# Shifting priorities by a table in a list-scheduled decoder layer, and a matmul price fitted to the measured rate

## The chip, the cores and the metric

The kernel runs on one core of one Trainium2 chip. The metric is device microseconds (us) of that core. The time before is the median of three timed runs; the profile comes from one further execution, whose own time is named beside its span below.

## The reference, cut to what matters

One decoder layer works on 1024 tokens of width 1024, with 16 learned tokens in front of them. Everything is float32. Four parallel branches (causal pooling, latent attention, a Conformer convolution, a short gated convolution) are merged by sigmoid gates.

```python
h = rms_norm(h_res, pre_norm_g[i])
z = h @ w_in[i]                         # 1024 -> 7328 columns, split among the branches
...
y_b = (mla_attention(...) * silu(mg)) @ w_out_mla[i]     # 8 heads, causal softmax
m = gts[0]*y_a + gts[1]*y_b + gts[2]*y_c + gts[3]*y_d
h_res = h_res + rms_norm(m @ w_o[i], post_norm_g[i])
return h_res[:, N_META:]
```

## The kernel before, in words

**Precision.** Each float32 operand is split into a high part, which TensorE can take, and a low rest (`split`: ScalarE copies, GpSimd or VectorE subtracts). A product is three matmuls: high by high, high by low, low by high. The two large products (`w_in` and `w_o`) are done by seven block products in place of eight.

**Three stages.** Stage one computes `z` and runs the convolution, pooling and the attention's inputs beside it. Stage two is attention (`maxima`, `attend`, `head_out`) in 16 units: 8 heads by 2 halves of the tokens. Between its matmuls stand 48 fills (`fills`, L1679): each is six matmuls of another branch's output product into a bank `y` of PSUM, followed on VectorE by a gating step that writes `th` and an addition to the running sum `m`. Stage three is the output: the attention branch's own output product (bank `u`, operand `boM`), then the product with `w_o`, whose results get a square on ScalarE, a gain multiply, a mean and a power on VectorE and GpSimd, and two closing VectorE operations per block of 128 tokens (`final`, L1899) before they are stored.

**In a unit of attention** (`attend`, L1583), each of 5 or 9 blocks of keys takes three matmuls into one of five banks `s`, a mask addition on VectorE on the diagonal, an exponential into `p32` and a copy into `pt` on ScalarE, a subtraction into `pt` on GpSimd (the low part), and three matmuls into the one bank `o`. At the end ScalarE copies bank `o` to `ol`. The row maxima of a later unit (`row_maxima`) also use the banks `s`; VectorE reduces them into `mxs`. `head_out` (L1660) scales `ol`, gates it and splits it into `boM`.

**What sets the order.** Nothing is issued while the program is written down. `record` (L324) stores each operation with its inputs' writers, a price from `cost` (L300) and a priority: its position in the record, less whatever `ahead` has lifted. The fills have their position plus 400. At the end of each stage `flush` (L363) plays the stage through: five engines, each of which, when free, starts the ready operation of the lowest priority number for which buffers are free; a price after that its results are due. In this order the instructions are then issued, and the chip's engines run them strictly in that order, each waiting for what it needs. So neither price nor priority changes what is computed; they change the order in which each engine, and each DMA queue, gets its instructions. In stage one, where the play finds TensorE idle, it also puts in small transposes that nobody reads (`keep_busy`).

The price of a matmul before is (L311):

```python
max(108, n / 2.25 + 3)        # n columns, in ns; also for a transpose
```

Of the kernel before, what the change touches and what calls it, by code (L numbers as in the profile page):

```python
# [21 lines left out]
F32 = mybir.dt.float32  # L22
# [191 lines left out]
class Plan:  # L214
# [6 lines left out]
    WAKE = {"PE": 350, "ACT": 150, "DVE": 150, "POOL": 150, "SP": 0}  # L221

    def __init__(self, nc):
        self.nc, self.ops, self.todo, self.lift, self.pipe = nc, [], [], 0, None
        self.after = 0
# [73 lines left out]
    @staticmethod  # L299
    def cost(eng, op, outs, ins, pow_):  # L300
        def size(v):
            return math.prod(v.shape[1:])
        if op == "dma_start":
            v, w = outs[0], ins[0]
            n = math.prod(v.shape) * 4
            run = 4 * min(v.shape[-1], w.shape[-1])
            return {"SP": 450, "ACT": 350, "POOL": 1000}[eng], n * (0.0235 + 35 / run) / 16
        n = max(size(v) for v in outs + [v for v in ins if isinstance(v, View)])
        if eng == "PE":
            n = size(outs[0])  # L310
            return (max(108, n / 2.25 + 3) if op == "transpose" or ins[0].dtype != F32 else max(430, 1.7 * n)), 0  # L311
        psum = any(isinstance(v, View) and v.buf.psum for v in outs + ins)
        if eng == "ACT":
            return (160 + 0.857 * n if psum else 200 + 0.83 * n), 0
        if op in ("memset", "affine_select"):
            return (60 if op == "memset" else 180) + 0.85 * n, 0
        if eng == "POOL":
            return (500 + 140 * n if pow_ else 180 + 2.2 * n), 0
        if op == "reciprocal":
            return 150 + 8.5 * n, 0  # L320
        both = psum and outs[0].buf.psum
        return 142 + (1.2 if op == "scalar_tensor_tensor" and (both or not psum) else 1.07) * n, 0
# [37 lines left out]
            return v.real() if isinstance(v, View) else v  # L360
        getattr(self.handle[o["eng"]], o["op"])(*map(real, o["args"]), **{k: real(v) for k, v in o["kw"].items()})  # L361

    def flush(self):  # L363

        self.lay_out()
        self.pipe = None
        ready = {e: [] for e in self.free}
        events, order = [], []
        for o in self.todo:
            o["need"] = 0  # L370
            o["at"] = 0
            for j in o["deps"]:
                d = self.ops[j]
                if d["end"] is None:
                    d["users"].append(o)
                    o["need"] += 1
                else:
                    o["at"] = max(o["at"], d["end"])
        for o in self.todo:
            if not o["need"]:  # L380
                heapq.heappush(events, (o["at"], 0, o["i"]))
        for e, t in self.free.items():
            heapq.heappush(events, (t, 1, 0))
        groups = {id(b.group): b.group for o in self.todo for b in o["bufs"] if b.group}
        for g in groups.values():
            for sl in g["slots"]:
                if sl["after"]:
                    heapq.heappush(events, (sl["after"], 1, 0))

        def slot(b, t):  # L390

            free = [sl for sl in b.group["slots"] if not sl["live"] and sl["after"] <= t]
            if free and (b.group["any"] or b.group["order"][b.group["next"]] is b):
                return min(free, key=lambda sl: (sl["after"], sl["i"]))

        def fits(o, t):

            if o["op"] == "dma_start" and o["eng"] != "POOL" and len(self.landed) >= 8 and self.landed[-8] > t:
                return False
            return all(slot(b, t) for b in o["bufs"] if not b.live and b.group)  # L400

        while events:
            t = events[0][0]
            while events and events[0][0] <= t:
                _, kind, i = heapq.heappop(events)
                if kind == 0:
                    o = self.ops[i]
                    bisect.insort(ready[o["eng"]], (o["prio"], o["i"]))
                elif kind == 2:
                    for b in self.ops[i]["bufs"]:  # L410
                        b.left -= 1
                        if b.left == 0 and b.group:
                            b.slot["live"], b.slot["after"] = None, t
            for e in self.free:
                if self.free[e] > t:
                    continue
                o = next((self.ops[i] for _, i in ready[e] if fits(self.ops[i], t)), None)
                if o is None:
                    if e == "PE" and self.idle and self.ops[self.idle[1]]["end"] is None:
                        self.row += 1  # L420
                        if self.row <= 8:
                            order.append(self.idle[0])
                        self.free[e] = t + 160
                        heapq.heappush(events, (self.free[e], 1, 0))
                    continue
                ready[e].remove((o["prio"], o["i"]))
                for b in o["bufs"]:
                    if not b.live:
                        b.live = True
                        if b.group:  # L430
                            b.slot = slot(b, t)
                            b.slot["live"] = b
                            b.group["next"] += 1
                o["start"] = t
                if e == "PE":
                    self.row = 0
                if o["turns"]:
                    o["cost"] += max(0, self.port[{"DVE": "POOL", "POOL": "DVE"}[e]] - t) * 0.7
                    self.port[e] = t + o["cost"]
                self.free[e] = t + o["cost"]  # L440
                o["end"] = t + o["cost"] + self.WAKE[e] + o["late"]
                if o["op"] == "dma_start":
                    if self.pipe is None:
                        self.pipe = max((x["done"] for x in self.ops if x["op"] == "dma_start"
                                         and "done" in x and x["start"] <= t), default=0)
                    o["done"] = self.pipe = max(self.pipe, t) + o["bytes"]
                    land = self.pipe + o["bytes"] + 4500 + min(0, o["extra"])
                    o["end"] = land + max(0, o["extra"])
                    if o["eng"] != "POOL":
                        self.landed.append(land)  # L450
                    heapq.heappush(events, (land, 1, 0))
                for b in o["bufs"]:
                    b.last = max(b.last, o["end"])
                order.append(o)
                heapq.heappush(events, (self.free[e], 1, 0))
                heapq.heappush(events, (o["end"], 2, o["i"]))
                for u in o["users"]:
                    u["need"] -= 1
                    same = u["eng"] == e and o["op"] != "dma_start"
                    u["at"] = max(u["at"], self.free[e] if same else o["end"])  # L460
                    if not u["need"]:
                        heapq.heappush(events, (u["at"], 0, u["i"]))
        if len(order) < len(self.todo):
            raise RuntimeError("no order: " + str([(o["eng"], o["op"], o["i"]) for o in self.todo if "start" not in o][:5]))
        for o in order:
            self.issue(o)
        self.todo = []


@with_exitstack  # L470
def trunk_kernel(ctx, tc, a):
# [10 lines left out]
    def ld(out, in_):  # L482
        SP.dma_start(f(out) if out.dtype == F32R else out, f(in_) if in_.dtype == F32R else in_)
# [13 lines left out]
    def split(hi, lo, src, eng=None):  # L497
        copy(hi, src)
        sub(eng or POOL, lo, src, f(hi))
# [1520 lines left out]
```

## Time and profile before

| | us |
|---|---|
| median of the three timed runs (965.73 to 969.6) | 968.28 |
| the profiled execution, its own time | 959.63 |
| its span | 957.9 |

TensorE works at a mean granted clock of 0.997. The stages, as the instructions show them: products with `w_in` and what runs beside them to about 629.5 us, attention to about 829.5 us, the output to the end. How to read the profile: PE is TensorE's matmuls and PEld its weight loads, which run ahead of the matmuls; DVE is VectorE, ACT ScalarE, POOL GpSimd, and SPq the queue that issues most DMAs. Matmuls are pipelined, so each record is longer than the distance from one start to the next. Nearly all operations carry line L361, the line in `issue` that hands them over, so groups are told apart by the tiles they write and read (`ps_s` is a bank `s`).

### The profile page before, as it was taken

To read this page: it belongs to the slowest core of one execution; us is meant where nothing else is said; L and a number is where in the kernel's file an instruction comes from. 1 tells how busy PE (TensorE), PEld (TensorE's weight loads), DVE (VectorE), ACT (ScalarE), POOL (GpSimd) and SP (SyncE) were. 2 spreads that over 40 slices of the span, in tenths; PEclk is the share of its full clock that TensorE was granted. 3 is DMA by queue.
4 is the path that set the end of the run, shared out by engine and by line. 5 is a ranking of instruction groups with operands and counts; after the bars stand their busy time and mean duration, and the time that the engine had idled before them with its cause. 6 is when DMAs were issued, how large, how long until landed. Compare 5 with 4: busy or idle time off the path is not lost.

```text
span 957.9 us, 15219 instructions
## 1 busy us (share of the span) xinstructions
PE 943.9 (99%) x4945; PEld 804.2 (84%) x4945; DVE 720.2 (75%) x1124; ACT 453.5 (47%) x925; POOL 677.7 (71%) x627
## 2 busy tenths in 40 slices
PE   8999999999999999999999999999999999999996
PEld 8998999988888888888888888888878878788885
DVE  6856979996999799547583657337778888799857
ACT  7752343434444445544454543266556565225632
POOL 5957669668787768669775977466467686738955
PEclk9999999999999999999999999999999999999998
DMA  8146566676779886788686678798978663783543
GB/s 262 46 126 198 151 202 196 211 224 204 249 229 280 281 283 209 244 224 245 221 255 187 191 243 279 220 300 259 294 207 275 199 184 111 264 266 107 189 141 144
DMA packets 143876, 205.96 MB, mean 215 GB/s; under 512 B 21169, under 2 KB 88752, under 8 KB 143028
## 3 DMA queue, kind: packets, MB, share of 16 engines
q1 hardware_dynamic: 134820, 188.20, 63.9%
q10 hardware_dynamic: 8656, 15.74, 4.5%
q8 instruction: 39, 0.64, 0.3%
q0 software_dynamic: 320, 1.05, 0.3%
q14 instruction: 41, 0.34, 0.1%
HBM read 132.01 MB, written 72.89 MB: 214 GB/s over the span
## 4 chain that ended last, share of the span: by engine, by line
PE 92%; DVE 3%; POOL 2%; issue 1%; ACT 1%; DMA 1%; SPq 0%; DVEq 0%; POOLq 0%; ACTq 0%
PE ps_pa L361 17%; PE ps_pb L361 17%; PE ps_pc L361 16%; PE ps_o L361 9%; PE ps_pd L361 8%; PE ps_u L361 7%; PE ps_s L361 7%; PE ps_y L361 6%; PE ps_x L361 4%; DMA x<-in_x_dram 1%; DVE th L361 1%; POOL pt L361 0%; ACT junk L361 0%; DVE op L361 0%; DVE c L361 0%
## 5 line engine op out<-in xcount | busy, mean ns | idle before, releaser
L361 PE MATMUL ps_pa<-B,A 128*128 128x512 f32 (+2 forms) x792 | 171.9, 359 | 0.0
L361 PE MATMUL ps_pb<-T,S 128*128 128x512 f32 (+2 forms) x792 | 170.7, 358 | 0.2 <-DVE u L361 0.2
L361 PEld LDWEIGHTS ps_pb<-T,S 128*128 128x128 f32 x792 | 134.4, 189 | 22.4 <-DVE u L361 0.4
L361 PEld LDWEIGHTS ps_pa<-B,A 128*128 128x128 f32 x792 | 134.2, 188 | 21.2 <-issue 0.2
L361 POOL TENSOR_TENSOR S<-ss,S 128x512 fp32r<-128x512 f32 x84 | 116.4, 1398 | 50.1 <-ACT S L361 43.3
L361 POOL TENSOR_TENSOR pt<-p,pt 128x512 fp32r<-128x512 f32 (+1 forms) x96 | 102.2, 1089 | 53.3 <-PE ps_s L361 27.4
L361 POOL TENSOR_TENSOR A<-raw,A 128x512 fp32r<-128x512 f32 x84 | 114.3, 1370 | 36.0 <-ACT A L361 35.7
L361 DVE TENSOR_TENSOR u<-ps_pb,u 128x512 f32<-128x512 f32 (+2 forms) x66 | 40.2, 610 | 67.3 <-PE ps_pb L361 62.2
L361 DVE SCALAR_TENSOR_TENSOR ps_w<-conv,par,ps_w 128x512 f32<-128x512 f32 x116 | 87.2, 752 | 2.5
L361 PE MATMUL ps_y<-bo,whl 128*128 128x512 f32 x288 | 84.6, 404 | 0.2 <-DVE th L361 0.2
L361 PE MATMUL ps_pd<-T,A 128*128 128x512 f32 (+2 forms) x396 | 84.5, 358 | 0.0
L361 PE MATMUL ps_pc<-T,S 128*128 128x512 f32 (+1 forms) x396 | 83.9, 357 | 0.0
L361 PE MATMUL ps_pc<-B,S 128*128 128x512 f32 (+1 forms) x396 | 83.7, 357 | 0.0
L361 ACT ACTIVATE S<-ss 128x512 fp32r<-128x512 f32 x84 | 50.2, 627 | 63.7 <-DVE ss L361 42.9
L361 ACT ACTIVATE p<-ps_s 128x512 f32<-128x512 f32 (+4 forms) x112 | 49.6, 444 | 61.2 <-PE ps_s L361 29.2
L361 PEld LDWEIGHTS ps_pd<-T,A 128*128 128x128 f32 x396 | 67.4, 188 | 10.9
L361 PEld LDWEIGHTS ps_pc<-B,S 128*128 128x128 f32 x396 | 66.9, 188 | 10.9
L361 PEld LDWEIGHTS ps_pc<-T,S 128*128 128x128 f32 x396 | 66.7, 189 | 11.0 <-issue 0.3
L361 PE MATMUL ps_o<-pt,vt 128*128 128x512 f32 (+7 forms) x288 | 68.9, 347 | 0.6 <-ACT ol L361 0.5
L361 PE MATMUL ps_s<-qt,kt 100*128 100x512 f32 (+4 forms) x336 | 68.7, 324 | 0.5 <-ACT p L361 0.5
L361 DVE TENSOR_TENSOR z<-ps_pc,u 128x512 f32<-128x512 f32 (+1 forms) x64 | 38.8, 606 | 33.9 <-PE ps_pc L361 27.4
L361 PEld LDWEIGHTS ps_s<-qt,kt 100*128 100x128 f32 (+1 forms) x336 | 54.1, 176 | 10.2 <-DVE qt L361 0.7
(298 smaller groups left out, 1924.7 us busy)
## 6 DMA issues: line engine op xcount, KB each, us to landing
raw<-in_w_in_dram SPq DMA_DIRECT2D x52, 512.0 KB
th<-th SPq DMA_DIRECT2D x32, 512.0 KB
th<-z ACTq DMA_DIRECT2D x60, 256.0 KB
v<-vhl SPq DMA_DIRECT2D x16, 384.0 KB
vt<-v SPq DMA_DIRECT2D x8, 768.0 KB
qt<-q SPq DMA_DIRECT2D x16, 384.0 KB
bo<-bo SPq DMA_DIRECT2D x6, 1024.0 KB
w_out_mla<-whl SPq DMA_DIRECT2D x16, 256.0 KB
```

The costliest lines, as they stand in the source:

```text
L361: getattr(self.handle[o["eng"]], o["op"])(*map(real, o["args"]), **{k: real(v) for k, v in o["kw"].items()})
```

## The change: what it does

Nothing is added to or taken from the computation. Three things change.

1. The price of a matmul of n columns becomes n·17/38.4 ns, plus 6 ns unless n is 512, and at least 30 ns. At 512 columns that is 226.7 ns, where the old formula gave 230.6; at 256 columns 119.3 (before 116.8); at 144 columns 69.8 (before 108); at 16 columns 30 (before 108). A transpose stays at 108. All three stages use it.
2. `flush` is taken apart into `simulate`, `commit` and a new `flush`. The rules of the play are the same.
3. In the second and third flush, a table adds a number to the priority of operations before the play. An entry (a, n, engine, by) means: of the n operations recorded from position a of the stage on, those of that engine (or all) get `by` added. A negative number moves an operation forward. There are 55 entries for attention and 7 for the output; none for stage one.

```diff
+SHIFTS = {
+    2: [
+        (515, 16, "PE", -400), (164, 16, "PE", 60), (1048, 32, None, -5), (1358, 64, "DVE", 5),
+        (1663, 8, None, 150), (1490, 64, "POOL", -5), (1072, 32, "DVE", -5), (1524, 16, "POOL", -150),
+        (1874, 2, None, 60), (144, 2, "PE", 20), (886, 16, "DVE", 5), (660, 16, "PE", 20), (1595, 32, "PE", -60),
+        (1866, 2, "PE", 150), (1322, 16, "DVE", -5), (1186, 8, "PE", -60), (1425, 8, None, -150),
+        (1014, 32, "DVE", -400), (1874, 4, "ACT", -60), (15, 4, "SP", -20), (1916, 4, None, -60),
+        (1936, 4, None, -20), (1299, 64, "PE", -5), (1492, 16, None, 20), (1323, 4, "DVE", 20), (1492, 1, None, 5),
+        (1642, 32, "PE", -5), (1090, 2, "DVE", 20), (1907, 32, "POOL", 400), (901, 1, "DVE", 400),
+        (1762, 16, "PE", -400), (1849, 32, None, -60), (1784, 16, "PE", 60), (182, 8, "PE", -400),
+        (1903, 8, "PE", 150), (1582, 4, "PE", 20), (1237, 1, None, -20), (252, 2, "DVE", 400),
+        (1491, 16, "PE", -150), (890, 64, "POOL", -20), (133, 8, "PE", -150), (980, 4, None, 5),
+        (1938, 2, None, 150), (1291, 4, "PE", -150), (1496, 64, "PE", 5), (968, 16, None, -20),
+        (1206, 32, "POOL", -400), (653, 64, "PE", -5), (1617, 32, "PE", 20), (1764, 32, "DVE", 60),
+        (1691, 8, "PE", -400), (1596, 64, "PE", -20), (1847, 16, "PE", 20), (1332, 2, None, -400),
+        (1218, 16, "PE", 20),
+    ],
+    3: [
+        (433, 16, "PE", -20), (139, 16, "POOL", 400), (860, 32, "DVE", -150), (814, 32, "PE", 60),
+        (600, 8, "PE", 60), (809, 16, "DVE", 400), (762, 2, None, -20),
+    ],
+}
...
-            return (max(108, n / 2.25 + 3) if op == "transpose" or ins[0].dtype != F32 else max(430, 1.7 * n)), 0
+            if op != "transpose" and ins[0].dtype == F32:
+                return max(430, 1.7 * n), 0
+            return (108 if op == "transpose" else max(30, n * 17 / 38.4 + (0 if n == 512 else 6))), 0
...
+        prio = {o["i"]: o["prio"] for o in ops}
+        self.phase += 1
+        for a, n, eng, by in SHIFTS.get(self.phase, ()):
+            for o in ops[a:a + n]:
+                if eng in (None, o["eng"]):
+                    prio[o["i"]] += by
+        r = self.simulate(prio, ops)
...
+        self.commit(r)
```

What some entries hit, counted along the record of the stage:

- attention, (15, 4, "SP", -20): four small loads, one row of ones for the second head's keys and three slices of the first head's values; they move in front of the loads of the first head's queries and keys.
- attention, (1524, 16, "POOL", -150) and the two small entries over the same place: the low part of one `pt` of the seventh head moves forward.
- attention, (1596, 64, "PE", -20) with (1642, 32, "PE", -5): among others one 272-column matmul of row maxima moves forward by 25.
- attention, (1849, 32, None, -60): among others the gating step of one of the last fills moves forward.
- attention, (1907, 32, "POOL", 400): the low parts of three of the last unit's `pt` move back by 400, behind the pending gating and splitting of earlier heads' outputs.
- output, (139, 16, "POOL", 400): three subtractions on GpSimd, the last of which is the low part of one operand `t2hl`.
- output, (814, 32, "PE", 60): twelve matmuls of the last block's `left` and the first two of the 256-column halves of `upper` for block 3 move back by 60, so that the second half of `upper` stands ahead of both.
- output, (809, 16, "DVE", 400) and (860, 32, "DVE", -150): VectorE's closing steps of block 2 move back, those of block 3 forward.

More of the change, by code (lines that the diff above doesn't have):

```diff
@@ L361, in issue, with simulate @@
         getattr(self.handle[o["eng"]], o["op"])(*map(real, o["args"]), **{k: real(v) for k, v in o["kw"].items()})
[L363 to L367, printed above, removed]
+    def simulate(self, prio, ops):
+        WAKE, free, port, landed = self.WAKE, dict(self.free), dict(self.port), list(self.landed)
+        need, at, end, start, cost = {}, {}, {}, {}, {}
+        left, live, slot_of, last = {}, set(), {}, {}
+        groups = {}
+        for o in ops:
+            for b in o["bufs"]:
+                if b not in left:
+                    left[b] = b.left
+                    if b.live:
+                        live.add(b)
+                        slot_of[b] = b.slot
+                    if b.group and id(b.group) not in groups:
+                        g = b.group
+                        groups[id(g)] = [g["next"], [[sl["live"], sl["after"], sl] for sl in g["slots"]], g]
+        for g in groups.values():
+            for sl in g[1]:
+                if sl[0] is not None and sl[0] not in left:
+                    left[sl[0]] = sl[0].left
+        ready = {e: [] for e in free}
         events, order = [], []
-        for o in self.todo:
-            o["need"] = 0
-            o["at"] = 0
+        for o in ops:
+            need[o["i"]], at[o["i"]] = 0, 0
+        for o in ops:
+            i = o["i"]
             for j in o["deps"]:
@@ L407, in flush @@
                     o = self.ops[i]
-                    bisect.insort(ready[o["eng"]], (o["prio"], o["i"]))
+                    bisect.insort(ready[o["eng"]], (prio[i], i))
                 elif kind == 2:
                     for b in self.ops[i]["bufs"]:
[L411 to L415, printed above, removed]
+                        left[b] -= 1
+                        if left[b] == 0 and b.group:
+                            sl = place[b] if b in place else next(x for x in groups[id(b.group)][1] if x[2] is slot_of[b])
+                            sl[0], sl[1] = None, t
+            for e in free:
+                if free[e] > t:
                     continue
@@ L418, in flush @@
                 if o is None:
[L419 to L424, printed above, removed]
+                    if e == "PE" and idle and end.get(idle[1], self.ops[idle[1]]["end"]) is None:
+                        row += 1
+                        if row <= 8:
+                            order.append((idle[0], None))
+                        free[e] = t + 160
+                        heapq.heappush(events, (free[e], 1, 0))
@@ L425, in flush @@
                     continue
-                ready[e].remove((o["prio"], o["i"]))
+                i = o["i"]
+                ready[e].remove((prio[i], i))
                 for b in o["bufs"]:
-                    if not b.live:
-                        b.live = True
+                    if b not in live:
+                        live.add(b)
                         if b.group:
-                            b.slot = slot(b, t)
-                            b.slot["live"] = b
-                            b.group["next"] += 1
@@ L434, in flush @@
-                o["start"] = t
+                            sl = place[b] = slot(b, t)
+                            slot_of[b] = sl[2]
+                            sl[0] = b
+                            groups[id(b.group)][0] += 1
+                start[i] = t
                 if e == "PE":
-                    self.row = 0
+                    row = 0
+                c = o["cost"]
                 if o["turns"]:
-                    o["cost"] += max(0, self.port[{"DVE": "POOL", "POOL": "DVE"}[e]] - t) * 0.7
-                    self.port[e] = t + o["cost"]
@@ L440, in flush @@
-                self.free[e] = t + o["cost"]
-                o["end"] = t + o["cost"] + self.WAKE[e] + o["late"]
-                if o["op"] == "dma_start":
[L443 to L448, printed above, removed]
+                    c += max(0, port[{"DVE": "POOL", "POOL": "DVE"}[e]] - t) * 0.7
@@ new lines, in simulate @@
+                    port[e] = t + c
+                cost[i] = c
+                free[e] = t + c
+                end[i] = t + c + WAKE[e] + o["late"]
+                if o["op"] == "dma_start":
+                    if pipe is None:
+                        pipe = max((x["done"] for x in self.ops if "done" in x and x["start"] <= t), default=0)
+                    pipe = max(pipe, t) + o["bytes"]
+                    o["done_"] = pipe
+                    land = pipe + o["bytes"] + 4500 + min(0, o["extra"])
+                    end[i] = land + max(0, o["extra"])
@@ L449, in flush @@
                     if o["eng"] != "POOL":
-                        self.landed.append(land)
+                        landed.append(land)
                     heapq.heappush(events, (land, 1, 0))
                 for b in o["bufs"]:
[L453 to L456, printed above, removed]
+                    last[b] = max(last.get(b, b.last), end[i])
@@ L457, in flush @@
+                order.append((o, pipe))
+                heapq.heappush(events, (free[e], 1, 0))
+                heapq.heappush(events, (end[i], 2, i))
                 for u in o["users"]:
-                    u["need"] -= 1
+                    k = u["i"]
+                    if k not in need:
+                        continue
+                    need[k] -= 1
                     same = u["eng"] == e and o["op"] != "dma_start"
-                    u["at"] = max(u["at"], self.free[e] if same else o["end"])
@@ L461, in flush @@
[L461 to L465, printed above, removed]
-            self.issue(o)
+                    at[k] = max(at[k], free[e] if same else end[i])
+                    if not need[k]:
+                        heapq.heappush(events, (at[k], 0, k))
+        if len(start) < len(ops):
+            return None
@@ new lines, in simulate, with commit @@
+        pe = max(start[o["i"]] + cost[o["i"]] for o in ops if o["eng"] == "PE")
+        return dict(order=order, start=start, end=end, cost=cost, left=left, live=live, slot_of=slot_of, last=last,
+                    groups=groups, free=free, port=port, landed=landed, row=row, pe=pe, stop=max(end.values()))
+    def commit(self, r):
+        for o, pipe in r["order"]:
+            if pipe is None and o.get("i") is None:
+                continue
+            i = o["i"]
+            o["start"], o["end"], o["cost"] = r["start"][i], r["end"][i], r["cost"][i]
+            if o["op"] == "dma_start":
+                o["done"] = pipe
+        for b, n in r["left"].items():
+            b.left = n
+            b.live = b in r["live"]
+            if b in r["slot_of"]:
+                b.slot = r["slot_of"][b]
+        for b, x in r["last"].items():
+            b.last = x
+        for nxt, slots, g in r["groups"].values():
+            g["next"] = nxt
+            for live, after, sl in slots:
+                sl["live"], sl["after"] = live, after
+        self.free, self.port, self.landed, self.row = r["free"], r["port"], r["landed"], r["row"]
+        for o, _ in r["order"]:
+            self.issue(o)
@@ new lines, in flush @@
+    def flush(self):
+        self.lay_out()
+        ops = self.todo
+        for o in ops:
+            for j in o["deps"]:
+                d = self.ops[j]
+                if d["end"] is None:
+                    d["users"].append(o)
+        prio = {o["i"]: o["prio"] for o in ops}
[5 more added lines that the diff above has]
+        r = self.simulate(prio, ops)
+        if r is None:
+            raise RuntimeError("no order")
+        self.commit(r)
```

37 lines of the change are left out of this document (20 added, 17 removed).

## Prediction, made before the changed kernel was run

> **What bounds the kernel now.** I read the page first, then the table of busy times by stretches, cut at the stage borders.
>
> ```profile
> PE 943.9 (99%) x4945; PEld 804.2 (84%) x4945; DVE 720.2 (75%) x1124; ACT 453.5 (47%) x925; POOL 677.7 (71%) x627
> PE 92%; DVE 3%; POOL 2%; issue 1%; ACT 1%; DMA 1%; SPq 0%; DVEq 0%; POOLq 0%; ACTq 0%
> ```
>
> ```profile
> 0.00:60.00 60.00, 56.69 (x458) 54.57 (x459) 41.25 (x67) 40.31 (x83) 41.93 (x52) 1.00 0.49 157
> 60.00:629.50 569.50, 569.26 (x2894) 485.68 (x2893) 419.03 (x576) 249.30 (x479) 412.92 (x373) 1.00 0.72 224
> 629.50:829.50 200.00, 198.12 (x1058) 164.41 (x1057) 156.19 (x354) 114.91 (x264) 140.19 (x142) 1.00 0.76 227
> 829.50:949.50 120.00, 119.87 (x541) 99.55 (x539) 98.62 (x121) 48.47 (x97) 79.21 (x58) 1.00 0.53 181
> 949.50:957.90 8.40, 0.00 (x0) 0.00 (x0) 5.09 (x9) 0.51 (x2) 3.40 (x4) 0.65 0.50 187
> ```
>
> TensorE is busy 99% of the span and carries 92% of the chain that ends last. The change removes no matmul, so it can gain only where TensorE waits. The columns after each stretch's length are PE, PEld, DVE, ACT, POOL. TensorE's idle time is 3.31 us in the first 60 us, 0.24 in the rest of stage one, 1.88 in attention, 0.13 in the output, and 8.4 after its last matmul. Stage one and the body of the output have nothing to give.
>
> A matmul's record stretches when it is held up briefly, so busy time hides short stops. The groups by shape show these:
>
> ```profile
> L361 PE MATMUL ps_u<-boM,whl 128*128 128x512 f32 x192 | 43.7, 389 | 0.0
> L361 PE MATMUL ps_y<-bo,whl 128*128 128x512 f32 x288 | 84.6, 404 | 0.2 <-DVE th L361 0.2
> L361 PE MATMUL ps_o<-pt,vt 128*128 128x512 f32 x96 | 35.0, 402 | 0.5 <-ACT ol L361 0.5
> L361 PE MATMUL ps_s<-qt,kt 100*128 100x512 f32 x48 | 19.3, 402 | 0.5 <-ACT p L361 0.5
> ```
>
> `ps_u` stands in the output, where nothing waits: 389 ns. The three attention groups of the same width average 404, 402 and 402. That is 288 x 15 + 96 x 13 + 48 x 13 = 6.2 us of stretching. With the 1.88 us that show as idle, some 8 us of attention could be order.
>
> Who holds TensorE up is read at the weight loads, which come first (view of waits, attention only; total, times, longest):
>
> ```profile
> PEld ps_s L361 <- ACT p L361: 1.2, 3, 0.7
> PEld ps_o L361 <- ACT ol L361: 1.2, 2, 0.9
> PEld ps_s L361 <- DVE mxs L361: 1.2, 2, 1.0
> PEld ps_y L361 <- DVE th L361: 0.9, 2, 0.6
> ...
> PEld ps_o L361 <- POOL pt L361: 0.3, 1, 0.3
> ```
>
> These are 4.8 us in ten waits, all for a buffer or an operand that another engine releases late.
>
> **The change part by part.**
>
> *The price.* The chain of waits has the output's first product as one unbroken piece:
>
> ```profile
> 829.54 43.52 PE ps_u L361 x192
> ```
>
> 43.52 / 192 = 226.7 ns a matmul, which the new price meets and the old one (230.6) misses by 3.9 ns. The price costs nothing on the chip; it moves what the play believes about TensorE relative to the others. In stage one, where no table acts, TensorE idles 0.24 us in 569.5, so a truer play has nothing to find. Another order there could add or remove a stall of the size of what is there: between -0.24 and, as my estimate, +0.9, which is the order of one wait in attention. In the first 60 us the 3.31 us of idle time are the arrival of the input, which no price moves, and the position of the throw-away transposes. I take 0 for stage one, with both ends kept.
>
> *The table in attention.* Of the ten waits, the table touches those for `mxs`, `th` and `pt`:
>
> ```profile
> 776.88 0.39 PE L361 MATMUL ps_s<-kt,qt 96*128 96x272 f32 x1 [0.55 <-DVE mxs L361]
> 827.88 1.23 PEld L361 LDWEIGHTS ps_y<-bo,whl 128*128 128x128 f32 x6 [0.61 <-DVE th L361]
> 712.23 0.96 PE L361 MATMUL ps_o<-pt,vt 128*128 128x512 f32 x3 [0.52 <-ACT ol L361]
> ```
>
> The matmul at 776.88 is the row-maximum one moved by 25, the gating step that releases 827.88 is moved by 60, and the low part that releases the short wait for `pt` goes forward by 150. These three sources make 1.2 + 0.9 + 0.3 = 2.4 us. The copy to `ol` and the exponentials `p` behind the other 2.4 us carry no shift where TensorE waits (712.23 is the longer of the two for `ol`). I take 2.0 of the 2.4, since a wait removed uncovers the next one. The lower bound is nothing. The upper is all 1.88 of idle time and three quarters of the 6.2 us of stretching: 6.5 us.
>
> Each moved step takes its followers along. A fill moved forward issues its two loads earlier too; they join the SP queue behind loads that were due long before. The four loads of entry (15, 4) pass the first head's keys:
>
> ```profile
> 617.99 0.32 SPq L361 DMA_DIRECT2D kt<-ones  x1
> 618.36 1.25 SPq L361 DMA_DIRECT2D vs<-v x3
> 629.62 2.93 PE L361 MATMUL ps_s<-qt,kt 96*128 96x512 f32 x17
> ```
>
> They take 1.57 us of the queue, and the keys are first used 11 us later: nothing, covered by the last products of stage one. Were that cover gone, it would cost 1.57 us.
>
> *The hand-over to the output.* GpSimd's queue there:
>
> ```profile
> 805.76 6.00 POOL L361 TENSOR_TENSOR pt<-p,pt 128x512 fp32r<-128x512 f32 x4 [5.20 <-PE ps_s L361]
> 811.72 1.75 POOL L361 TENSOR_TENSOR op<-op,smg 128x512 f32<-128x512 f32 x1
> 813.43 3.92 POOL L361 TENSOR_TENSOR pt<-p,pt 128x512 fp32r<-128x512 f32 x4
> 817.31 1.29 POOL L361 TENSOR_TENSOR boM<-op,boM 128x512 fp32r<-128x512 f32 x1
> 818.56 1.74 POOL L361 TENSOR_TENSOR op<-op,smg 128x512 f32<-128x512 f32 x1
> 821.11 1.35 POOL L361 TENSOR_TENSOR boM<-op,boM 128x512 fp32r<-128x512 f32 x1 [0.52 <-ACT boM L361]
> 830.78 1.29 POOL L361 TENSOR_TENSOR boM<-op,boM 128x512 fp32r<-128x512 f32 x1 [0.74 <-ACT boM L361]
> ```
>
> From 805.76 GpSimd hardly rests until the last `boM` at 832.07. The output's first product starts at 829.54 and comes to the second half's last `boM` after 12 + 9 matmuls, at 829.54 + 21 x 0.2267 = 834.3: a slack of 2.2 us. Three of the four `pt` at 813.43 are put behind what else is pending, by +400. At least the two `boM` and the `op` between them pass (1.29 + 1.74 + 1.35 = 4.4 us); with the two `op` of the next head (I price each at 1.74) 7.9 us. The last unit's `ps_o`, its `ol` and so the last `boM` would come that much later. Fills cover TensorE until 829.5, and behind the slack 2.2 to 5.7 us would be bare. I take 0, since GpSimd takes a moved-back step as soon as it has nothing else ready, and the two `boM` wait for ScalarE first; both ends are kept.
>
> *The table in the output.* TensorE never waits in its body, so a gain can only lie in the last 8.4 us. The entry on `t2hl` moves three GpSimd steps behind whatever else is ready there; GpSimd is busy 79 of the output's 120 us, so they still run when its queue next runs dry, some steps before TensorE wants them: nothing, and one step of 1.75 us (811.72 above) if that cover is gone. The tail:
>
> ```profile
> 947.77 1.60 PE L361 MATMUL ps_o<-wa,B 128*128 128x256 f32 x12
> 950.95 0.15 DVE L361 TENSOR_SCALAR rso<-rso 128x1 f32<-128x1 f32 x1
> 951.22 0.72 POOL L361 TENSOR_TENSOR g<-a,pgB 128x256 f32<-128x256 f32 x1
> 951.91 0.99 POOL L361 TENSOR_TENSOR rso<-rso,mhalf 128x1 f32<-128x1 f32 x1
> 953.41 0.74 DVE L361 SCALAR_TENSOR_TENSOR c<-c,rso,xr 128x512 f32<-128x512 f32 x1
> 954.08 0.73 DVE L361 SCALAR_TENSOR_TENSOR g<-g,rso,xr 128x512 f32<-128x512 f32 x1
> ```
>
> With the second half of block 3 ahead of `left`, its gain step (951.22, 0.72 us) leaves the end. The power, ready at 951.10, then starts about 0.8 us sooner, and two closing steps and a store follow it as before. Gain 0.8 us; at most 1.2, if the power also runs without its neighbour. The loss is bounded by a collision on the way:
>
> ```profile
> 944.84 0.75 DVE L361 SCALAR_TENSOR_TENSOR u<-u,rso,xr 128x512 f32<-128x512 f32 x1 [0.33 <-POOL rso L361]
> 945.40 1.33 POOL L361 TENSOR_TENSOR a<-a,pgB 128x512 f32<-128x512 f32 x1 [0.60 <-ACT junk L361]
> 945.51 1.78 DVE L361 SCALAR_TENSOR_TENSOR c<-c,rso,xr 128x512 f32<-128x512 f32 x1
> ```
>
> The same step took 0.75 us alone and 1.78 beside a GpSimd step that began 0.11 us before it: one more such meeting costs 1.03 us. [...]
>
> *Sum*: 0 - 2.0 + 0 + 0 - 0.8 = -2.8 us. Against the profiled execution that is 959.6 - 2.8 = 956.8 (span 957.9, about 1.7 around it). The timed runs lie at 965.7 to 969.6, median 968.3, some 8.6 us above the profiled one, which no view explains; I leave that difference as it is and forecast **965.5 us**.
>
> **The rivals.**
>
> *The short stops go too.* If the play now keeps every operand ahead of TensorE, the upper bound holds: 6.5 + 0.8 = 7.3 us, giving 961.0. For it: the stretching is spread over hundreds of matmuls, and 55 entries reorder much. Against: most shifted steps are not those at which TensorE is seen to stop. [...]
>
> *Exchange.* The waits removed return elsewhere, and the tail meets one collision: -2.4 + 2.4 - 0.8 + 1.0 = +0.2, giving 968.5. For it: the order is exact to a few hundred ns only, and the longest waits have no shift on their releasers.
>
> *GpSimd takes over at the hand-over.* The moved-back `pt` delay the last `boM`, up to +5.7 with nothing gained elsewhere: 974.0. It decides from a delay of 2.2 us, the slack above. For it: GpSimd's rows above follow one another with hardly a gap. Against: TensorE's fills can be placed into the hole.
>
> *The change does nothing of the kind*, because the order hardly differs: 968.3; it falls in with exchange.
>
> **How the numbers follow.** About 0.5% (4.8 us) is what a measurement of this kernel can tell from no change. The forecast and exchange lie within it, and so does about a fifth of the first rival. Chances: forecast 0.38, short stops 0.32, exchange 0.18, hand-over 0.12. Faster by over 0.5%: four fifths of 0.32 and some of the forecast's upper edge, 0.29. Slower: 0.12, since the hand-over passes the bound only near its upper end, and I let stage one's unknown order fill it up. Within: 0.59. The range reaches from 7.3 + 1.2 us of gain (the first rival with 0.24 from stage one, 0.4 more from the tail and some of the last quarter of stretching), 959.8, to a little over the middle of the hand-over's 968.3 to 974.0, 971.5.
>
> **What would show it.** Right: the waits of weight loads in attention fall from 4.8 to about 2.8 us, for `mxs` and `th` above all; attention's stretch is near 198 us; the output's matmuls are as dense as before; the 256-column `ps_o` stands ahead of the last 512-column ones, and less than 8 us follow the last matmul. Wrong: idle time of TensorE at the first `ps_u` or in stage one; record lengths of `ps_y` falling to 390 (first rival), or staying while the list of waits only changes its names (exchange).

## The result, and the profile after

The changed kernel takes 962.62 us (median of 6 executions, 961.49 to 964.39); the kernel before, beside it, 967.2 (6 executions, 962.33 to 969.6). The ratio is 0.995, 95% interval 0.9929 to 0.9971: 4.6 us faster, inside the predicted range, 2.9 us under the forecast. The profiled executions say the opposite: 961.49 us after (span 959.6) against 959.63 before (span 957.9). The edit alone cannot have done both, and most of what follows is about this.

Busy times by stretches of the changed kernel (PE, PEld, DVE, ACT, POOL, as before):

```profile
60.00:629.50 569.50, 568.49 (x2893) 485.32 (x2892) 408.80 (x575) 248.05 (x479) 409.13 (x373) 1.00 0.71 223
629.50:829.50 200.00, 196.89 (x1052) 163.69 (x1050) 153.48 (x352) 114.03 (x264) 139.43 (x141) 1.00 0.77 228
829.50:949.50 120.00, 120.00 (x540) 99.35 (x539) 90.07 (x117) 47.60 (x93) 81.77 (x59) 1.00 0.53 184
```

TensorE's idle time in stage one went from 0.24 to 1.01 us, in attention from 1.88 to 3.11. The output stays full. The cuts are those of before, while attention now runs from 630.5 to 831.1 us; it started at 629.4 and ended at 829.4 before. Stage one's new idle time has one owner, among the profile's costliest groups (idle time and its releaser are at the end):

```profile
L389 PE MATMUL ps_pb<-T,S 128*128 128x512 f32 (+2 forms) x792 | 171.0, 358 | 1.0 <-DVE u L389 1.0
```

That wait, at 145 us, was 0.2 before. The groups of attention, by shape:

```profile
L389 PE MATMUL ps_u<-boM,whl 128*128 128x512 f32 x192 | 43.8, 390 | 0.0
L389 PE MATMUL ps_y<-bo,whl 128*128 128x512 f32 x288 | 86.3, 405 | 0.0
L389 PE MATMUL ps_o<-pt,vt 128*128 128x512 f32 x96 | 35.4, 398 | 2.5 <-ACT ol L389 2.1 <-POOL pt L389 0.3
```

The fills are as long as before (404 then, 405 now), `ps_o` is 4 ns shorter, and it now has a stop of 2.1 us. The waits of the weight loads in attention:

```profile
PEld ps_o L389 <- ACT ol L389: 2.6, 1, 2.6
PEld ps_o L389 <- POOL pt L389: 1.5, 4, 0.6
PEld ps_s L389 <- ACT p L389: 0.9, 2, 0.7
...
PEld ps_o L389 <- ACT pt L389: 0.7, 2, 0.5
...
PEld ps_y L389 <- DVE th L389: 0.2, 1, 0.2
```

The waits for `mxs` are gone and those for `th` fell from 0.9 to 0.2. In their place stand more waits for `pt` (0.3 before, 2.2 now) and one long one for `ol`. The kinds shown sum to 4.8 us before and 5.9 after. The whole list goes from 6.1 to 7.6: the prediction's ten waits had left out three for `qt` (0.7 before, 0.2 now) and two short ones. ScalarE's timeline shows what holds `ol`:

```profile
640.52 0.60 ACT L389 ACTIVATE ol<-ps_o 128x512 f32<-128x512 f32 x1 [2.83 <-DMA th<-zlast]
```

`zlast` is the last output of stage one. GpSimd issued its store at 632.43, and the first `ol` of attention lies in the memory that this store still reads. The store took 8.0 us to land. Before, it was issued at 631.33 and took 3.6 us, and the same copy ran at 636.94 without a wait.

The tail, from VectorE's timeline:

```profile
951.27 0.42 DVE L389 TENSOR_TENSOR a<-ps_u,a 128x256 f32<-128x256 f32 x1
951.61 0.14 DVE L389 TENSOR_REDUCE rso<-sso 128x1 f32<-128x4 f32 x1
951.79 0.15 DVE L389 TENSOR_SCALAR rso<-rso 128x1 f32<-128x1 f32 x1
951.86 1.11 DVE L389 TENSOR_TENSOR g<-a,pgB 128x256 f32<-128x256 f32 x1
952.89 0.74 DVE L389 SCALAR_TENSOR_TENSOR a<-a,rso,xr 128x512 f32<-128x512 f32 x1
953.55 0.14 DVE L389 TENSOR_REDUCE rso<-sso 128x1 f32<-128x4 f32 x1
...
955.81 0.75 DVE L389 SCALAR_TENSOR_TENSOR g<-g,rso,xr 128x512 f32<-128x512 f32 x1
```

### The profile page after: what moved, and what is told of

Read it like the earlier page. It is cut to its first block, busy times and chain, and to the rows that moved or that the text cites. A ratio compares the mean times of both kernels' runs of the same rounds, so it can differ in the third digit from the quotient of the medians.

```text
span 959.6 us, 15213 instructions
## 1 busy us (share of the span) xinstructions
PE 943.1 (98%) x4944; PEld 803.2 (84%) x4944; DVE 700.4 (73%) x1124; ACT 451.8 (47%) x925; POOL 675.7 (70%) x627
## 4 chain that ended last, share of the span: by engine, by line
PE 91%; DMA 2%; DVE 2%; issue 1%; POOL 1%; ACT 1%; SPq 0%; DVEq 0%; ACTq 0%; POOLq 0%
PE ps_pa L389 16%; PE ps_pb L389 15%; PE ps_pc L389 14%; PE ps_o L389 10%; PE ps_y L389 8%; PE ps_u L389 8%; PE ps_pd L389 7%; PE ps_s L389 7%; PE ps_x L389 4%; DVE ps_w L389 1%; DMA kt<-k 1%; DMA x<-in_x_dram 1%; SPq L389 0%; POOL S L389 0%; DMA th<-z 0%
## 5 line engine op out<-in xcount | busy, mean ns | idle before, releaser
L389 PE MATMUL ps_pa<-B,A 128*128 128x512 f32 (+2 forms) x792 | 169.2, 358 | 0.0
L389 POOL TENSOR_TENSOR pt<-p,pt 128x512 fp32r<-128x512 f32 (+2 forms) x96 | 104.3, 1112 | 46.7 <-PE ps_s L389 24.6
L389 PE MATMUL ps_s<-qt,kt 100*128 100x512 f32 (+7 forms) x336 | 68.6, 323 | 0.6 <-ACT p L389 0.6
L389 ACT ACTIVATE z<-z,par 128x512 f32<-128x512 f32 x45 | 32.5, 721 | 66.2 <-DVE z L389 65.3
L389 PEld LDWEIGHTS ps_s<-qt,kt 100*128 100x128 f32 (+2 forms) x336 | 54.4, 176 | 10.8 <-ACT p L389 0.9
```

## The experiments

The first question was whether the 4.6 us belong to the price, to the table, or to the occasion. On each occasion below the kernel before ran beside the others on the same chip; its values there come first.

**First occasion of its own: the parts alone, and both kernels again.** Kernel before: 960.62 us (29 executions, 959.64 to 965.57), not 967.2.

The kernel before as a copy:

> The kernel before, unchanged, as a second copy. Theory scatter (the executions of before differ among themselves by 7 us, 962.3 to 969.6, and part of the measured 0.5% is that): the copy's ratio to before lies off 1 by up to 0.3%, its runs spread over 5 us or more, and the profile of another execution shows where such an execution loses time. Theory order (the new order is really shorter and the profile shown of before was a lucky execution): the copy's ratio is 1.000 within 0.15%, and its profile has about 4 us more waits of TensorE than the first profile of before.

Measured: 960.55, ratio 0.9994 (0.9979 to 1.0008). The ratio is that of a copy, but neither theory's sign is there: the spread is 3.7 us, and TensorE is busy 198.10 us of attention's 200, as in the first trace (198.12).

The new price with an empty table:

```diff
-SHIFTS = {2: [...], 3: [...]}
+SHIFTS = {}
```

> The new price of a matmul, the table empty. Theory price (a truer play of all stages is the gain): ratio near 0.995, most of the -4.6 us. Theory table (the shifts are the gain): ratio near 1.000, 966 to 968 us, with attention about 200 us long. My forecast's split (attention -2.0 and tail -0.8 from the table, price 0) expects 0.999 to 1.001.

Measured: 963.72, ratio 1.0025 (1.0013 to 1.0038). The price alone costs, which none of the three expectations had. TensorE's stops in its trace are the one at 145 us, one of 0.9 us behind `ol` as above, a new one of 0.8 us for an operand `qt`, and the old ones.

The table with the old price:

```diff
-            return (108 if op == "transpose" else max(30, n * 17 / 38.4 + (0 if n == 512 else 6))), 0
+            return (max(108, n / 2.25 + 3) if op == "transpose" or ins[0].dtype != F32 else max(430, 1.7 * n)), 0
```

> The table of shifts, the price of a matmul as before. Theory table: ratio 0.995 to 0.998 if the shifts act by themselves. Theory price: 1.000 or slower, since the shifts were written for the order that the new price gives and meet another one here: up to +3 us.

Measured: 971.57, ratio 1.0102 (1.0079 to 1.0124). Without the price the table costs 11 us, far over the 3 us expected, most of it in attention (208.5 us long, where it was 200.0), with a stop for a load, behind which the clock stood at half from 738.33 to 741.74:

```profile
737.06 0.40 PE L387 MATMUL ps_s<-kt,qt 96*128 96x348 f32 x1 [1.89 <-DMA qt<-q]
```

The changed kernel as a copy:

> The changed kernel, unchanged, beside the other three on one chip. Theory order: ratio 0.995 again, spread of the runs under 3 us. Theory scatter: ratio anywhere from 0.994 to 0.999. A second profile shows whether the 2.3 us wait of TensorE early in attention and the 1.2 us wait at 145 us belong to the order or to that one execution.

Measured: 962.77, ratio 1.0013 (1.0000 to 1.0025). Its own time is that of the result (962.62); it is the kernel before that stands 6.6 us lower. Here the change is 2 us slower, which neither theory had. The main difference between this trace of the changed kernel and the first is shown by the stretches after its stop for `ol` (the last three columns are granted clock, DMA share and GB/s):

```profile
638.00:642.61 4.61, 2.12 (x13) 1.49 (x11) 1.06 (x4) 1.38 (x4) 1.29 (x1) 1.00 1.00 411
642.61:646.02 3.41, 3.41 (x11) 2.52 (x10) 0.96 (x3) 2.67 (x5) 2.51 (x2) 0.50 0.99 279
```

After a stop of 2.49 us TensorE's clock was at half for 3.41 us. The first trace had 2.12 us of stop and no such stretch. The mean clocks of the executions go with their times. Of the kernel before, beside the runs of three occasions (86 executions; one more, of 3338 us, is left out):

```
mean granted clock   executions   median us
0.998                27           960.5
0.997                30           960.6
0.996                17           963.6
0.995 and less       12           967.0
```

Of the 29 executions at 0.996 and less, 27 took over 962.5 us; of the other 57, six did. A line through the 86 rises by 1.45 us for each 0.001 of clock lost. One stretch of 3.41 us at half lowers the mean by 3.41 x 0.5 / 960 = 0.0018, so by this line each goes with about 2.6 us. That it is the stop ahead of the stretch and the slow matmuls in it is an estimate: it comes from how clock and time go together, not from a trace of a long execution. The kernel before has a quiet level of 960.5 us and executions above it, more on some occasions than on others. Each occasion was on another chip, so chip and occasion cannot be told apart here.

**Second occasion: where stage one and attention meet.** Kernel before: 963.26 (35 executions, 959.74 to 969.78).

The changed kernel with `ol` laid elsewhere, every engine's order unchanged:

```diff
-    for n, tag in ((2, 'ol'),):
+    for n, tag in ((1, 'rb'), (1, 'op0'), (2, 'ol')):
```

> The changed kernel with one line altered: the tile rb and the tile op0 are laid ahead of ol in attention's memory, so that ol no longer lies where the last output of stage one (zlast) is stored from. Every engine's order is that of the changed kernel. Theory: the stop of TensorE of 2.3 to 2.7 us at 639 us is the copy to ol waiting for the store of zlast to land, and it is this stop that sets the clock to half for 3.4 us in some executions. Without it: no wait of ps_o for ol at 639 us, granted clock 0.997 to 0.998 in every execution, and a time 2.5 to 3.5 us under the changed kernel's 962.8, that is 0.4 to 1.5 us under the kernel before. Rival: the copy waits for something else there (the first ps_o behind its operands), or the next operand is as late; then the time stays within 0.7 us of the changed kernel's, 1.5 to 2.5 us over the kernel before.

Measured: 962.40 (959.37 to 965.63), ratio 0.9989 (0.9963 to 1.0015). The wait for `ol` is gone from the trace; the clocks are not all at 0.997, and the median is only 0.4 under the changed kernel's on the other occasions, as the rival has it. The first half of the theory is borne out, that the store holds `ol`; the other half fell: the next operand was late, the weights of the first fill, and two more stops followed:

```profile
647.37 0.47 PE L389 MATMUL ps_y<-bo,whl 128*128 128x512 f32 x1 [1.75 <-DMA whl<-w_out_pool]
649.45 0.54 PE L389 MATMUL ps_s<-kt,qt 96*128 96x328 f32 x2 [0.74 <-DMA qt<-q]
660.10 1.06 PE L389 MATMUL ps_s<-kt,qt 96*128 96x144 f32 x4 [1.92 <-issue]
```

Behind the last one the clock stood at half from 660.40 to 663.82.

Old price in stage one, new price and table after it (the line stands in `record`):

```diff
+        if self.phase == 0 and eng == "PE" and (op == "transpose" or ins[0].dtype != F32):
+            cost = max(108, math.prod(outs[0].shape[1:]) / 2.25 + 3)
```

> The changed kernel, but stage one is laid out with the old price; the new price and the table act in attention and the output. Theory: stage one then has neither the stop of 1.2 us at 145 us (it goes back to 0.4) nor the order that puts ol's first copy behind the store of zlast, so the time is 1.5 to 2.5 us under the kernel before. Rival: the table fits only the state in which the new price leaves stage one, as it cost 11 us on the old price; then it is over the kernel before by 2 us or more.

Measured: 965.90, ratio 1.0028 (1.0009 to 1.0047). The rival holds: on another state at the end of stage one the table costs more than it brings.

The same with the table empty:

```diff
-SHIFTS = {2: [...], 3: [...]}
+SHIFTS = {}
```

> Stage one with the old price, attention and the output with the new one, the table empty. Theory: the table is what shortens the waits of attention, so this stands 0.5 to 1.5 us over the kernel before (price alone was 3.2 us over it, of which 0.8 is the stop at 145 us and 1.1 the one for ol). Rival: the price is what helps once stage one leaves it alone; then it is as fast as the run with the table, 1 us or more under the kernel before.

Measured: 960.53 (960.16 to 962.47), ratio 0.9972 (0.9949 to 0.9994). Neither expectation fits fully: it is no faster than the quiet level of the kernel before, but it stays there where that does not. Why it stays there, no run shows. Against the run before it, the table costs 5.4 us here.

The new price everywhere, no table, `ol` elsewhere:

```diff
-SHIFTS = {2: [...], 3: [...]}
+SHIFTS = {}
...
-    for n, tag in ((2, 'ol'),):
+    for n, tag in ((1, 'rb'), (1, 'op0'), (2, 'ol')):
```

> The new price everywhere, the table empty, ol laid elsewhere as in the first of these runs. Theory: of the 3.2 us that the price alone costs, the stop of 1.1 us for ol goes, so 1.8 to 2.4 us over the kernel before; the table is then worth 2.5 to 3.5 us against the first of these runs. Rival: the table is worth only the 1 us seen so far, and both runs with ol elsewhere lie within 1.2 us of each other.

Measured: 962.09 (961.38 to 964.91), ratio 0.9987 (0.9965 to 1.0009). Over the quiet level of 960.5 it is 1.6, where the price with `ol` in the old place was 3.2: without the table the place of `ol` costs about 1.6 us, counted over two occasions (with the table it was 0.4). Against the run with the table (962.40) it differs by 0.3, as the rival has it: the table is worth little by the median.

**Third occasion: two more traces of the kernel before,** unchanged, in the hope of a long execution.

> The kernel before, unchanged, for the trace of one more execution. Its executions on one chip went from 959.7 to 969.8 us, at mean granted clocks from 0.998 down to 0.992, about 1.5 us more for each 0.001 of clock. Theory: a longer execution is one in which loads of attention land late, TensorE stops for about 2 us, and its clock then stands at half for 3.4 us (which lowers the mean by 0.0018); so if this one takes over 963 us, its trace shows at least one such stretch of half clock inside attention with a stop ahead of it, and stage one and the output as in the other traces. If it takes 960 to 961.5 us, there is none. Rival: longer executions are slower all over, a few tenths of a per cent in each stage.

Measured: 960.76, at a clock of 0.998.

> The same as the look before it, another execution: over 963 us with a stop and a stretch of half clock in attention, or 960 to 961.5 us with none; by the rival a longer time with every stage longer.

Measured: 959.41, at 0.997. One more execution beside them, without a trace, took 963.07 at 0.997. Both traces are quiet, with no stretch of half clock ahead of the tail. They say nothing on the long executions, so the theory went untested for the kernel before.

**Fourth occasion: the changed kernel once more, unchanged, and the version that stayed quiet** (old price in stage one, new price after it, table empty). Kernel before: 961.4 (22 executions, 959.59 to 966.91; the execution of 3338 us is the one left out).

> The changed kernel, unchanged, beside the kernel before on one more occasion. On one occasion it was 4.6 us under the kernel before, on another 2.2 us over it; its own time was 962.6 and 962.8, and the kernel before's was 967.2 and 960.6. Theory: the changed kernel is about 2 us longer wherever the kernel before runs undisturbed, and its gain is nothing but executions of the kernel before in which TensorE is stopped and its clock halved; so its median is 962 to 963.5 again, and the ratio follows the kernel before: over 1.001 if that has its median under 961.5 at mean clocks of 0.997 to 0.998, under 0.997 if that has it over 965 with most clocks at 0.996 or less. Rival: the changed kernel moves with the kernel before, and the ratio is that of one of the two occasions whatever the clocks.

Measured: 962.84 (961.5 to 963.62), ratio 1.0009 (0.9994 to 1.0024). The third time within 0.3 us of 962.6, whatever the kernel before does. In this trace the copy to `ol` did not have to wait for the store, and the stop stood at the fill instead:

```profile
647.26 0.47 PE L389 MATMUL ps_y<-bo,whl 128*128 128x512 f32 x1 [2.37 <-DMA whl<-w_out_pool]
649.47 0.54 PE L389 MATMUL ps_s<-kt,qt 96*128 96x328 f32 x2 [0.86 <-DMA qt<-q]
```

```profile
644.60:649.96 5.36, 2.13 (x10) 1.32 (x9) 0.74 (x2) 2.85 (x9) 2.74 (x5) 1.00 1.06 199
649.96:653.37 3.41, 3.41 (x14) 3.19 (x13) 1.63 (x5) 1.23 (x2) 0.56 (x1) 0.50 1.03 267
```

> The price of before in stage one, the new price in attention and the output, no table: the run of this kind that stood at 960.5 in 12 executions (960.2 to 962.5) where the kernel before stood at 963.3 (959.7 to 969.8). Theory: its work is no shorter than that of the kernel before, which has 960.3 when nothing stops it, but its order leaves the loads more room, so it stays at 960 to 961.5 here too, 1.5 us or more under the changed kernel, and under the kernel before by as much as that is disturbed. Rival: it was chance, and it spreads as the kernel before does on this occasion.

Measured: 960.52 (959.79 to 961.45), ratio 0.9986 (0.9973 to 1.0000). With the run of the same kernel on the second occasion that makes 24 executions between 959.8 and 962.5, all but one at 0.997 or 0.998. It is 2.3 us under the changed kernel on the same chip, the best of all versions tried, and no shorter than a quiet execution of the kernel before.

## Why the prediction was right or wrong

**The number** was inside the range by luck, not for its reasons. My sum of -2.8 us was made against the quiet profiled execution; there the change brought +1.9 (961.49 - 959.63), and against the quiet level of the later occasions about +2.3 (962.8 - 960.5). The 4.6 us of the result lie in the step that I left as it was: the 8.6 us by which the timed runs stood above the profiled one, "which no view explains". They are executions of the kernel before above its quiet level. On that occasion five of six were over 962.5 us and the sixth took 962.33 (967.2 - 960.5 = 6.7, which the line above would put down to two to three half-clock stretches); on the later occasions 6 of 29, 19 of 35 and 8 of 22 were over 962.5. That the long executions run at lower mean clocks is measured on the later occasions; for the six of the result the clocks are not on record, and no long execution of the kernel before has a trace. Where in it TensorE stops, and why so often on that occasion, stays open.

**Stage one, 0 (-0.24 to +0.9):** the idle time rose by 0.8, close to the upper end. It is the one wait for `u` at 145 us; with the old price in stage one it is back at 0.2. My estimate of one wait in size was right; that "a truer play has nothing to find" did not exclude that it loses something. With the slower start of that trace, attention begins 1.1 us later than in the first trace of before. The start of the trace adds differences that are no part of the change: TensorE's idle time in the first 60 us is 3.31, 3.55, 4.59 and 2.83 us in four traces of the kernel before, and 4.03 after.

**Attention, -2.0:** this step failed, and the exchange rival is what the traces show, with a loss on top. From its first matmul to the first `ps_u`, attention takes 199.97 to 200.08 us in the four traces of the kernel before, and 200.6, 201.9 and 202.6 in the three of the changed kernel, where I had 198. The two sources that I tied to entries did go: `mxs` and `th` from 2.1 to 0.2. The third, `pt`, moved against me, and `ol` cost more than all that was won. In the first trace TensorE idles 1.2 us more in attention than before. The wait for `ol` I had listed as one that no entry touches, and so as one that would stay at 1.2. I looked for what moves within the stage; this one comes over the border of stages: a later store, a buffer laid over its source, and a play that lets the copy start at 635.32 us of its own clock where it lets the store land at 635.31, while on the chip landing took 8.0 us from the issue at 632.43. The first rival, that the short stops go too, is refuted by the fills' 405 ns.

**The loads, "nothing":** I priced the moved loads by the SP queue (1.57 us) and let the last products of stage one cover them. Of the four loads of entry (15, 4), the three slices of values did not pass the keys: each is written over zeros that have to land first, and in the first trace they go out at 624.18, behind the first head's queries and keys (607.03 to 612.93), where they went out at 618.36 before. What was short was the landing of a later load. SyncE's queue in the changed kernel on the fourth occasion, and in the kernel before:

```profile
633.46 0.43 SPq L389 DMA_DIRECT2D vt<-v  x1
633.99 1.00 SPq L389 DMA_DIRECT2D bo<-bo  x2
635.08 0.73 SPq L389 DMA_DIRECT2D whl<-w_out_pool  x1
```

```profile
623.89 0.42 SPq L361 DMA_DIRECT2D vt<-v  x1
631.94 0.93 SPq L361 DMA_DIRECT2D bo<-bo  x2
632.91 0.55 SPq L361 DMA_DIRECT2D whl<-w_out_pool  x1
```

The first fill takes these weights at 647.26 in the one, 12.2 us after their issue and after a wait of 2.37; in the other at 643.46, after 10.6 us and without a wait. With `ol` elsewhere it was 12.8 us and a wait of 1.75. So the room between issue and use did not shrink; the landing grew from at most 10.6 us to over 12. The DMA engines are full there in both kernels (shares 0.99 to 1.06 in the rows above, 0.99 before from 630 to 641 us), so that alone is not the difference. The load of `vt` (768 KB) goes out right ahead of these in the changed kernel, 8 us ahead before. Whether it is what delays them no run tests. In the other two traces of the changed kernel the weights were in time, with TensorE already held up by `ol`.

**Hand-over, 0:** right. The three `pt` went behind a gating and a split, as worked out, and the output's first product stands in one piece:

```profile
831.34 43.56 PE ps_u L389 x192
```

43.56 / 192 is 226.9 ns a matmul, and TensorE is busy 120.00 of the stretch's 120.00 us. The GpSimd rival is refuted.

**Output, 0, and the tail, -0.8:** the body is as dense as before. The gain in the tail was mis-sized: it changed by -0.1. The 256-column `ps_o` went ahead, and the gain step left the end, as I said. But VectorE took up the room: its product `g` ran beside a GpSimd step for 1.11 us where it had taken 0.41, and a closing step of 0.74 at 952.89 stood ahead of the reduction on which the last power waits. From the end of the last matmul (949.64 + 1.59 = 951.23; its row, as that before, has 12 of 256 columns) to the end of the last VectorE step (956.56) it is 5.33 us; before, 954.81 - 949.37 = 5.44. I had taken only GpSimd off the path, not what stands ahead of that reduction on VectorE.

**The signs.** Of the signs named ahead, the place of the 256-column `ps_o` and the dense output came out right; the waits at 2.8 us (5.9), an attention near 198 us (200.6) and less than 8 us behind the last matmul (959.6 - 951.2 = 8.4) did not.

## What to carry to other kernels

When timed runs stand several us above the profiled one, that gap is a term of the sum and not an offset: list each execution's mean clock before attributing a gain to an edit, and run the old kernel again. An order fitted to one state (the table) need not be worth anything on a neighbouring state: here the same table was worth -0.3 to 1.0 us on its own base, and cost 5 and 11 us on two others. At a border between stages, look for a buffer laid over one that a store still reads, and price a load by its landing, which here took from under 10.6 to 12.8 us for the same 256 KB, and not only by the time that its issue takes of the queue.

## What the runs showed of the hardware that was not expected

TensorE's granted clock stood at half behind some stops of about 2 us and not behind others. In four traces a stretch of 3.41 us at half followed a stop of 1.89, 1.92, 2.37 (and 0.86 more) or 2.49 us; stops of 2.12 and 1.75 us in two traces were followed by none. So the length of the stop alone does not tell these cases apart. Nor does TensorE's busy time around it (it stands behind the length). The first row below has the 2.49 us on the first occasion and ends where half clock begins; the other two are the 2.12 us of the changed kernel's first trace and what follows:

```profile
639.20:642.61 3.41, 0.92 (x5) 0.58 (x4) 0.57 (x2) 1.29 (x3) 0.31 (x1) 1.00 1.02 418
```

```profile
638.45:641.86 3.41, 1.29 (x6) 0.75 (x5) 0.89 (x3) 1.31 (x3) 0.66 (x1) 1.00 1.01 419
641.86:645.27 3.41, 3.06 (x19) 2.32 (x18) 1.37 (x4) 3.31 (x7) 2.93 (x3) 1.00 1.07 270
```

In the 3.41 us ahead of the other three stretches TensorE is busy 1.49, 1.53 and 1.84 us, more than the 1.29 that full clock followed. Matmul records are longer than the distance between starts (`ps_u`: 389 ns against 226.7), so the busy times are rough. What decides whether half clock follows a stop, the runs do not show.

The store of one buffer, issued by GpSimd, took more than twice as long to land in one execution as in another. The last store of `zlast` (256 KB) took 3.6 us in the first trace of the kernel before, and 8.0, 8.4 and 3.9 us in the three of the changed kernel, whose order is the same in all three.
